# Queries and keys of a mixer take the seven-product form for a third pair of k tiles, with two sets of sums moved earlier

## The chip, the cores and the metric

The kernel runs on one core of one Trainium2 chip, as one launch. The metric is the device time of that launch in microseconds. Each multiplication of the layer is in float32 precision, made on TensorE (PE) out of rounded parts: an operand x is split into a high part (x rounded to fp32r, a cast on ScalarE, ACT) and a low part (x minus the high part, on VectorE, DVE), and a product is summed from three matmuls, high x high, high x low and low x high.

## The reference, cut to what matters

```
x = x + 1/2 * swiglu(rms_norm(x, ffn1_norm), w_gate, w_up, w_down)       # first FFN
h = rms_norm(x, mix_norm);  proj = h @ w_in                              # 256 x 2048 times 2048 x 4112
u, q, k, v, g, a_lr = split(proj, IN_SPLITS)                             # 1024 | 512 | 512 | 1024 | 1024 | 16
x = x + concat(pool(u), gla(q, k, v, g, a_lr)) @ w_out
x = x + cross_attention(rms_norm(x), rms_norm(mem))
x = x + 1/2 * swiglu(rms_norm(x, ffn2_norm), ...);  out = rms_norm(x, final_norm)
```

256 tokens, width 2048, FFN width 5632. The change concerns the end of the first FFN and the 1024 columns q | k of `proj`.

## The kernel before

**Units.** A weight matrix is read in units of 1 MB: 256 rows of k (two "k tiles", called a pair; pairs 0 to 7 cover k = 2048) by 1024 columns. `Stream` keeps a list of units and of operations between them. When unit u is emitted, units up to u + 2 have been split into parts (`AHEAD = 2`), and the split of a unit issues the load of the unit three further on (`RAW = 3` buffers of raw weights). `st.op(f, n)` puts f behind the n-th unit that follows. `in_turn` makes each weight-split instruction of an engine queue behind the one before it; `among_weights` puts other work at a place in that same order, and `issue_after` orders a block behind one instruction.

**Plain and seven-product units.** A plain unit (`unit_p`) is 2 k tiles x 2 column halves x 2 token halves x 3 matmuls = 24 matmuls of 128 x 128 by 128 x 512. Its split is one cast on ACT (wh, 2048 wide) and one subtraction on DVE (wl). A seven-product unit (`unit_s`, `split_seven`) treats the pair as a 2 x 2 block matrix and needs 7 block products of 3 matmuls = 21. For it the raw blocks w0..w3 are added up to four sums in the tile T (three DVE operations, line 488), three raw blocks are split into xh and xl (1536 wide), and the four sums into wh (two casts) and wl. The activations need sums of their own for that pair, made once per pair by `Sums.make` (lines 426 to 438 on DVE, then a cast and a subtraction). The banks of PSUM that hold the seven products' own sums are joined by `combine` (lines 583 to 588) behind the last seven-product unit of a block. PSUM has four tiles (`bufs=4`): a block of `block_s` takes two for its whole sums and two for the parts until `combine` has read them.

**Around the change.** The last part of the first FFN's down product ends with six plain units (`block_t`, columns 1024 to 2047). `into_x` puts behind the first unit that follows: `fold(2)` and `fold(3)`, which transpose the new x on PE (line 802), scale it and split it into `xs` (ACT line 248, DVE line 240) and square it (line 811); one unit later `finish_norm` (sums, Rcol, diag), and `spread_norm` (line 233, two spreads) seven units after the block's end. Then the first mixer block multiplies `xs` by the q | k columns in the order `ORDER_IN = (0, 2, 4, 1, 5, 3, 6, 7)` of pairs, with pairs 1 and 3 in the seven-product form. In what follows u0 to u7 are its eight units in the order of execution; before, u3 (pair 1) and u5 (pair 3) are the seven-product ones. Between u6 and u7 runs the low-rank unit (`low_rank`, line 1077, 16 matmuls into a PSUM tile of its own, `split_a` for its weights). The activations' sums for pairs 1 and 3 are made in the last FFN units, those for pair 5 two units behind the q | k block; they lie in free parts of `ys`. The next block (the pool columns) has again pairs 1 and 3 as seven-product units, and the v and gate blocks have 1, 3 and 5. In the scope of the mixer (`s_mix`) T, xh and xl have one buffer each. The instruction order of each engine is fixed when the program is built, from the order of the code, the constraints named above, and a simulated time.

Of the kernel before, what the change touches and what calls it, by code (L numbers as in the profile page):

```python
# [14 lines left out]
P = 128  # L15
# [5 lines left out]
NB = 512  # L21
# [78 lines left out]
def build(ctx, tc, I, out):  # L100
# [11 lines left out]
    def open_scope(name, shared=None):  # L112


        def f():
            scope["shared"] = shared or {}
            scope["stack"] = ExitStack()
            scope["pool"] = scope["stack"].enter_context(
                tc.tile_pool(name=name, bufs=1, reuse_waits="tile")
            )  # L120
        return f

    def shared_tile(tag, n, dt, name, bufs):

        homes = scope["shared"].get(tag)
        if homes:
            homes.append(homes.pop(0))
            tag, size, bufs = homes[-1]
        else:
            size = n  # L130
        return scope["pool"].tile([P, size], dt, tag=tag, name=name, bufs=bufs)[:, :n]
# [125 lines left out]
    def in_turn(engine, f):  # L257

        if engine in latest:
            with tc.issue_after(latest[engine].ins):  # L260
                latest[engine] = f()
        else:
            latest[engine] = f()
# [6 lines left out]
    def among_weights(f):  # L270
# [4 lines left out]
        if scalar is not None:  # L275
            latest["scalar"] = scalar

    def split_weights(hi, lo, src):
        in_turn("scalar", lambda: nc.scalar.copy(hi, src))  # L279
        in_turn("vector", lambda: nc.vector.tensor_tensor(  # L280
            out=lo, in0=src, in1=f32(hi), op=ALU.subtract
        ))
# [16 lines left out]
    def finish_norm(n, spread_too=True):  # L299

        nc.vector.tensor_reduce(out=sums, in_=ss[:, :, :n], axis=AX.X, op=ALU.add)
        done = rsqrt(Rcol, sums, D, 2)
        if spread_too:
            diag["R"] = [diagonal(Rcol[:, t : t + 1]) for t in range(2)]
        return done
# [60 lines left out]
    def block_t(srcs, act, evict, delays=(0, 0), amid=None):  # L366

        n_k = 2 * len(srcs)  # L370
        held = {}

        def unit(gi):
            def fn(wh, wl):
                if gi == 0:
                    held["ps"] = [ptile(uid("pt")) for _ in range(2)]
                wh, wl = (w.rearrange("p (k j n) -> p k j n", j=2, n=NB) for w in (wh, wl))
                quarters = [(j, kk) for j in range(2) for kk in range(2)]
                if amid is not None and gi == 0:
                    quarters.sort(key=lambda q: q[1])  # L380
                for n, (j, kk) in enumerate(quarters):
                    if amid is not None and n == (1 if gi else 3):
                        amid(gi)
                    k = 2 * gi + kk
                    for h in range(2):
                        products(held["ps"][j][:, h, :], act, k, h, wh[:, kk, j], wl[:, kk, j],
                                 k == 0, k == n_k - 1)
            return fn

        for gi, src in enumerate(srcs):  # L390
            st.unit(src, unit(gi))
        for j in range(2):
            st.op(lambda j=j: evict(j, held["ps"][j]), delays[j])
# [6 lines left out]

    def jtile():
        return tmp.tile([P, NB], F32, tag="j", name=uid("j"))

# [64 lines left out]
        f.clump = True  # L470
        return f

    def split_seven(u, raw, shared):

        t = shared_tile("T", 4 * NB, F32, f"T{u}", 1)
        w = raw.rearrange("p (b n) -> p b n", n=NB)
        v = t.rearrange("p (b n) -> p b n", n=NB)
        th, tl = (
            wpool.tile([P, 4 * NB], F32R, tag=n, name=f"{n}{u}", bufs=st.AHEAD + 1)
            for n in ("wh", "wl")  # L480
        )
        rh, rl = (shared_tile(n, 3 * NB, F32R, f"{n}{u}", 2) for n in ("xh", "xl"))
        for o, a, b in (
            (v[:, 0:2], w[:, 1:3], w[:, 0:1].to_broadcast([P, 2, NB])),
            (v[:, 2], v[:, 0], w[:, 2]),
            (v[:, 3], v[:, 2], w[:, 3]),
        ):
            in_turn("vector", lambda: nc.vector.tensor_tensor(out=o, in0=a, in1=b, op=ALU.add))  # L488
        split_weights(rh, rl, raw[:, NB:])
        for c in (slice(0, 2 * NB), slice(2 * NB, 4 * NB)):  # L490
            in_turn("scalar", lambda: nc.scalar.copy(th[:, c], t[:, c]))  # L491
        low_parts(tl, t, th, shared)
        return [[x.rearrange("p (b n) -> p b n", n=NB) for x in (th, tl, rh, rl)]], None
# [271 lines left out]
    def residual(scale, b, last=1):  # L765

        def evict(j, ps):
            x = x_cols((2 * b + j) * NB, NB)
            nc.vector.scalar_tensor_tensor(
                out=x, in0=ps, scalar=scale, in1=x, op0=ALU.mult, op1=ALU.add  # L770
            )
            if j == last:
                store_x(b)
        return evict
# [57 lines left out]
    END = IntoX((0,), None, None, None)  # L832

    def into_x(w, act, scale, gain=None, k0=0, nk=KT, spread_too=True, src=None, way=OUTPUT,
               spread_at=3, behind=None):

        for b in range(2):
            st.op(lambda b=b: fetch_x(b, src), 2)
            cols = wwide(w, b * 2 * NB, k0, nk)
            if way.sevens[b]:  # L840
                block_s(cols, act, way.sums, way.orders[b], residual(scale, b, 0),
                        early_parts(scale, b), way.sevens[b], behind=None if b else behind)
            else:
                block_t(cols, act, residual(scale, b))
            if gain is not None:
                for j in range(2):
                    st.op(lambda c=2 * b + j: fold(c, gain), way.folds[2 * b + j])
        if gain is not None:
            st.op(lambda: finish_norm(4, spread_too), way.folds[3] + 1)
            if spread_too:  # L850
                st.op(spread_norm, spread_at)

# [99 lines left out]
    def down_first(wd, k0, nk, last, way):  # L952
        way.make_sums()
        if last:
            for g, after in zip(qk_sums.pairs[:2], (9, 11)):
                st.op(lambda g=g: among_weights(lambda: qk_sums.make(g)), after)
        into_x(wd, ys, 0.5, G_MIX if last else None, k0, nk, src=None if k0 else I["x"][0],
               way=way, spread_at=7)

    ffn(I["ffn1_w_gate"][0], I["ffn1_w_up"][0], I["ffn1_w_down"][0], down_first,  # L960
        amid_first)
    st.op(close_scope, 1)
    MIX_HOMES = {"T": [("T", D, 1)], "xh": [("xh", 3 * NB, 1)], "xl": [("xl", 3 * NB, 1)]}
    st.op(open_scope("s_mix", MIX_HOMES), 1)


    w_in = I["w_in"][0]
# [303 lines left out]
    def low_rank():  # L1271
        st.unit(load_a, a_unit, split_a)
        st.op(ev_a)

    block_s(wwide(w_in, 2 * NB), xs, qk_sums, ORDER_IN, ev_qk, home=wide_home, amid={6: low_rank},
            sevens=(1, 3))
    st.op(lambda: turn_qk(1), 1)
    st.op(lambda: turn_qk(0), 2)
    st.op(lambda: among_weights(lambda: qk_sums.make(5)), 2)
    st.op(decay, 2)  # L1280
    def head(h):
        attend(h)
# [6 lines left out]
    def queries_of(*hs):  # L1289
        for h in hs:  # L1290
            st.op(lambda h=h: behind_weights(lambda: queries(h)))

    block_s(wwide(w_in, 0), xs, qk_sums, ORDER_IN, ev_pool, home=wide_home,
            behind={0: (0, decay_logits)}, sevens=(1, 3),
            amid={4: lambda: queries_of(0, 1), 6: lambda: scores_of(0, 1)})
    for f, h, after in (
# [2 lines left out]
        (head, 0, 9), (head, 1, 9), (head, 2, 10), (head, 3, 10), (lambda _: head_norms(), None, 15),  # L1299
    ):  # L1300
        st.op(lambda f=f, h=h: f(h), after)
    def raw_parts_in(high, low):
        of = {n: [(n, 3 * NB, 1), home, (n, 3 * NB, 1)] for n, home in (("xh", high), ("xl", low))}
        return lambda: scope["shared"].update(of)

    st.op(raw_parts_in(("v", 4 * NB, 1), ("m4", 8 * S, 1)))
    block_s(wwide(w_in, 4 * NB), xs, qk_sums, ORDER_IN, ev_v, home=v_home)
    st.op(raw_parts_in(("v", 4 * NB, 1), ("kq", 4 * LINES, 1)))
# [382 lines left out]
    st.op(close_scope)  # L1691


    raws = {}

    def load(u):
        raws[u] = wpool.tile([P, 4 * NB], F32, tag="raw", name=f"raw{u}", bufs=st.RAW)
        st.units[u][0](raws[u])

    def split_unit(u, own, shared):  # L1700
        raw = raws.pop(u)
        if own is split_seven:
            return split_seven(u, raw, shared)
        parts = [
            wpool.tile([P, 4 * NB], F32R, tag=t, name=f"{t}{u}", bufs=st.AHEAD + 1)
            for t in (("wh",) if own else ("wh", "wl"))
        ]
        if own:
            own(parts[0], raw)
            return parts, None  # L1710
        hi, lo = parts
        step = {0: NB, 1: 2 * NB, 2: 2 * NB}.get(u, 4 * NB)
        for c in range(0, 4 * NB, step):
            part = slice(c, c + step)
            if u == 0 and c in (step, 2 * step):
                latest["scalar"] = rows["parts", 0, c // step - 1][0]
            if step < 4 * NB:
                split_weights(hi[:, part], lo[:, part], raw[:, part])
            else:
                in_turn("scalar", lambda: nc.scalar.copy(hi, raw))  # L1720
                low_parts(lo, raw, hi, shared)
        return (hi, lo), None
# [39 lines left out]
```

## Time and profile before

| | |
|---|---|
| time, median of 3 runs | 2072.26 us (2072.12 to 2073.15) |
| the profiled execution's own time | 2072.4 us |
| its span, first to last instruction | 2070.6 us |
| granted TensorE clock, mean | 0.999 |
| matmuls | 9464 |
| VectorE busy / ScalarE busy | 1843.2 us / 1173.4 us |

The profile is one execution, taken by the hardware profiler. A line of a timeline begins with the start and the duration in us, then engine, source line, operation, output and inputs by the program's tile names, their size and the count; what stands in brackets is the engine's idle time before it and what ended it. The chain is the work that ended last, followed back from the end; its pieces follow each other without a gap.

### The profile page before, as it was taken

To read this page: it belongs to the slowest core of one execution; us is meant where nothing else is said; L and a number is where in the kernel's file an instruction comes from. 1 tells how busy PE (TensorE), PEld (TensorE's weight loads), DVE (VectorE), ACT (ScalarE), POOL (GpSimd) and SP (SyncE) were. 2 spreads that over 40 slices of the span, in tenths; PEclk is the share of its full clock that TensorE was granted. 3 is DMA by queue.
4 is the path that set the end of the run, shared out by engine and by line. 5 is a ranking of instruction groups with operands and counts; after the bars stand their busy time and mean duration, and the time that the engine had idled before them with its cause. 6 is when DMAs were issued, how large, how long until landed. Compare 5 with 4: busy or idle time off the path is not lost.

```text
span 2070.6 us, 24069 instructions
## 1 busy us (share of the span) xinstructions
PE 2059.8 (99%) x9464; PEld 1714.1 (83%) x9464; DVE 1843.2 (89%) x1720; ACT 1173.4 (57%) x1196; POOL 103.6 (5%) x93
## 2 busy tenths in 40 slices
PE   9999999999999999999999999999999999999998
PEld 7888888888888888888888888888888888888886
DVE  7998899989998779989889877989988999889987
ACT  7654455554554666665755544656554565545554
POOL 0000000000000000000000000000000010000001
PEclk9999999999999999999999999999999999999999
DMA  7666766566666655467655455666577765676664
GB/s 265 205 203 224 243 214 215 184 228 236 226 201 224 228 182 183 164 205 277 228 183 188 160 181 183 203 224 221 171 238 222 236 213 185 224 242 223 209 226 154
DMA packets 123129, 435.92 MB, mean 211 GB/s; under 512 B 9860, under 2 KB 13544, under 8 KB 122632
## 3 DMA queue, kind: packets, MB, share of 16 engines
q1 hardware_dynamic: 122840, 434.12, 62.6%
q8 instruction: 74, 1.21, 0.2%
q14 instruction: 39, 0.32, 0.0%
q10 hardware_dynamic: 176, 0.27, 0.0%
HBM read 417.58 MB, written 16.78 MB: 210 GB/s over the span
## 4 chain that ended last, share of the span: by engine, by line
PE 99%; DVE 0%; DMA 0%; ACT 0%; issue 0%; SPq 0%; POOL 0%; POOLq 0%; DVEq 0%; ACTq 0%
PE pt L362 64%; PE pt L509 30%; PE ph L791 2%; PE pl L1416 1%; PE pv L1453 1%; PE px L802 1%; PE pp L1049 0%; DMA x<-in_x 0%; PE pa L1077 0%; PE tm L1362 0%; PE po L1215 0%; PE px L728 0%; PE pq L1202 0%; PE pe L362 0%; DVE wl L455 0%
## 5 line engine op out<-in xcount | busy, mean ns | idle before, releaser
L362 PE MATMUL pt<-wh,xs 128*128 128x512 f32 x2432 | 780.9, 391 | 0.0
L1720 ACT CAST wh<-raw 128x2048 fp32r<-128x2048 f32 x242 | 461.7, 1912 | 228.4 <-PE pt L362 128.3
L455 DVE TENSOR_TENSOR wl<-raw,wh 128x2048 fp32r<-128x2048 f32 (+1 forms) x242 | 515.7, 2140 | 82.9 <-ACT wh L1720 82.7
L362 PEld LDWEIGHTS pt<-wh,xs 128*128 128x128 f32 x2432 | 455.9, 188 | 94.4 <-issue 0.5
L491 ACT CAST wh<-T 128x1024 fp32r<-128x1024 f32 x264 | 277.0, 1054 | 380.6 <-DVE T L488 359.6
L362 PE MATMUL pt<-wl,xs 128*128 128x512 f32 x1216 | 474.1, 390 | 0.0
L362 PE MATMUL pt<-wh,ys 128*128 128x512 f32 x1452 | 458.0, 389 | 0.0
L362 PEld LDWEIGHTS pt<-wh,ys 128*128 128x128 f32 x1452 | 272.5, 188 | 56.3
L455 DVE TENSOR_TENSOR wl<-T,wh 128x2048 fp32r<-128x2048 f32 (+1 forms) x132 | 296.7, 2247 | 5.6 <-ACT wh L491 5.2
L362 PE MATMUL pt<-wl,ys 128*128 128x512 f32 x726 | 283.0, 390 | 0.0
L362 PEld LDWEIGHTS pt<-wl,xs 128*128 128x128 f32 x1216 | 228.5, 188 | 46.2
L280 DVE TENSOR_TENSOR xl<-raw,xh 128x1536 fp32r<-128x1536 f32 x132 | 231.1, 1751 | 13.9 <-ACT xh L279 13.8
L279 ACT CAST xh<-raw 128x1536 fp32r<-128x1536 f32 x132 | 195.4, 1480 | 60.6 <-PE pt L509 38.6
L488 DVE TENSOR_TENSOR T<-T,raw 128x512 f32<-128x512 f32 x264 | 182.1, 690 | 6.8
L488 DVE TENSOR_TENSOR T<-raw 128x1024 f32<-128x1024 f32 x132 | 160.7, 1217 | 0.6
L362 PEld LDWEIGHTS pt<-wl,ys 128*128 128x128 f32 x726 | 136.3, 188 | 28.0
L509 PE MATMUL pt<-xh,xs 128*128 128x512 f32 x416 | 154.9, 389 | 0.0
L509 PE MATMUL pt<-wh,xs 128*128 128x512 f32 x396 | 153.9, 389 | 0.0
L459 POOL TENSOR_TENSOR wl<-raw,wh 128x768 fp32r<-128x768 f32 x44 | 81.8, 1858 | 1390.9 <-DVE wl L455 1368.1
L509 PE MATMUL pt<-wh,xe 128*128 128x512 f32 x320 | 124.3, 389 | 0.0
L509 PEld LDWEIGHTS pt<-xh,xs 128*128 128x128 f32 x416 | 78.1, 188 | 16.2
L509 PEld LDWEIGHTS pt<-wh,xs 128*128 128x128 f32 x396 | 74.3, 188 | 15.4
(274 smaller groups left out, 2081.7 us busy)
## 6 DMA issues: line engine op xcount, KB each, us to landing
raw<-in_ffn_w_down SPq DMA_DIRECT2D x88, 1024.0 KB, 5.5
raw<-in_ffn_w_up SPq DMA_DIRECT2D x80, 1024.0 KB, 5.1
raw<-in_ffn_w_gate SPq DMA_DIRECT2D x77, 1024.0 KB, 5.1
raw<-in_w_in SPq DMA_DIRECT2D x32, 1024.0 KB, 5.1
raw<-in_xattn_w_kv SPq DMA_DIRECT2D x32, 1024.0 KB, 5.0
raw<-in_w_out SPq DMA_DIRECT2D x16, 1024.0 KB, 6.6
raw<-in_xattn_w_q SPq DMA_DIRECT2D x16, 1024.0 KB, 5.6
raw<-in_xattn_w_o SPq DMA_DIRECT2D x16, 1024.0 KB, 5.6
```

The costliest lines, as they stand in the source:

```text
L279: in_turn("scalar", lambda: nc.scalar.copy(hi, src))
L280: in_turn("vector", lambda: nc.vector.tensor_tensor(out=lo, in0=src, in1=f32(hi), op=ALU.subtract))
L362: latest["product"] = nc.tensor.matmul(ps, a, w, start=first and i == 0, stop=last and i == 2)
L455: in_turn("vector", lambda: nc.vector.tensor_tensor(out=lo[:, :n], in0=src[:, :n], in1=f32(hi[:, :n]), op=ALU.subtract))
L459: rest = nc.gpsimd.tensor_tensor(out=lo[:, n:], in0=src[:, n:], in1=f32(hi[:, n:]), op=ALU.subtract)
L488: in_turn("vector", lambda: nc.vector.tensor_tensor(out=o, in0=a, in1=b, op=ALU.add))
L491: in_turn("scalar", lambda: nc.scalar.copy(th[:, c], t[:, c]))
L509: nc.tensor.matmul(banks[n], x, w, start=n in fresh and j == 0, stop=n in ends and j == 2)
L791: rows["turned"] = nc.tensor.transpose(v[:, i, h * P : (h + 1) * P], g[:, h, i * P : (i + 1) * P], ident)
L802: nc.tensor.transpose(v[:, j, h * P : (h + 1) * P], x[:, h, j * P : (j + 1) * P], ident)
L1416: nc.tensor.matmul(ps[:, t, :M], ys[:, 4 * h + d, a, tok], xa["K", h][:, d, b, :], start=i == 0, stop=i == 11,)
L1720: in_turn("scalar", lambda: nc.scalar.copy(hi, raw))
```

## The change

1. The q | k block has the order (0, 2, 4, 1, 6, 3, 5, 7) and takes pairs 1, 3 and 5 in the seven-product form, so u4 is pair 6 (plain) and u6 is pair 5 (seven products).
2. The activations' sums for pair 5 are made behind u3 of this block, not two units behind its end.
3. `split_seven` is cut in two: `sum_blocks` (the three additions into T) and the rest. For u3 `sum_blocks` is an operation of its own, ahead of `fold(2)`, `fold(3)` and `finish_norm`, in place of behind them; `finish_norm` is ordered behind it. The scope of the mixer is opened one unit sooner for this.
4. In this block the homes of xh and xl go in turns: their own tile for u3, a part of `ys` for u5, their own tile again for u6.

```diff
@@ shared_tile
             homes.append(homes.pop(0))
+            if callable(homes[-1]):
+                return homes[-1]()
             tag, size, bufs = homes[-1]
@@
+    def behind_sums(f):
+        with tc.issue_after(latest["sums"].ins):
+            f()
@@
-    def split_seven(u, raw, shared):
-        t = shared_tile("T", 4 * NB, F32, f"T{u}", 1)
+    def sum_blocks(u):
+        raw = raws[u]
+        t = block_sums[u] = shared_tile("T", 4 * NB, F32, f"T{u}", 1)
...
         for o, a, b in (
             (v[:, 0:2], w[:, 1:3], w[:, 0:1].to_broadcast([P, 2, NB])),
             (v[:, 2], v[:, 0], w[:, 2]),
             (v[:, 3], v[:, 2], w[:, 3]),
         ):
             in_turn("vector", lambda: nc.vector.tensor_tensor(out=o, in0=a, in1=b, op=ALU.add))
+        latest["sums"] = latest["vector"]
+
+    def split_seven(u, raw, shared):
+        if u not in block_sums:
+            sum_blocks(u)
+        t = block_sums.pop(u)
...
@@ into_x(..., sums_of=None), called with sums_of=3 for the last part of the first FFN
+            if b and sums_of:
+                st.op(lambda u=len(st.units) + sums_of: sum_blocks(u), way.folds[2])
             if gain is not None:
                 for j in range(2):
                     st.op(lambda c=2 * b + j: fold(c, gain), way.folds[2 * b + j])
         if gain is not None:
-            st.op(lambda: finish_norm(4, spread_too), way.folds[3] + 1)
+            norm = lambda: finish_norm(4, spread_too)
+            st.op((lambda: behind_sums(norm)) if sums_of else norm, way.folds[3] + 1)
@@
-    st.op(close_scope, 1)
+    st.op(close_scope)
...
-    st.op(open_scope("s_mix", MIX_HOMES), 1)
+    st.op(open_scope("s_mix", MIX_HOMES))
@@
-    block_s(wwide(w_in, 2 * NB), xs, qk_sums, ORDER_IN, ev_qk, home=wide_home, amid={6: low_rank},
-            sevens=(1, 3))
+    def raw_parts_in_ys():
+        return raw_parts_in(*(
+            lambda i=i: ys[:, 3 * i : 3 * i + 3].rearrange("p k a s -> p (k a s)") for i in range(2)
+        ))
+
+    def third_sums():
+        st.op(lambda: among_weights(lambda: qk_sums.make(5)))
+
+    st.op(raw_parts_in_ys())
+    block_s(wwide(w_in, 2 * NB), xs, qk_sums, (0, 2, 4, 1, 6, 3, 5, 7), ev_qk, home=wide_home,
+            amid={3: third_sums, 6: low_rank})
     st.op(lambda: turn_qk(1), 1)
     st.op(lambda: turn_qk(0), 2)
-    st.op(lambda: among_weights(lambda: qk_sums.make(5)), 2)
     st.op(decay, 2)
@@ ahead of the pool block
+    st.op(lambda: scope["shared"].update({n: [(n, 3 * NB, 1)] for n in ("xh", "xl")}))
@@ split_unit (raws now stands further up)
-        raw = raws.pop(u)
+        raw = raws[u]
```

More of the change, by code (lines that the diff above doesn't have):

```diff
@@ L393, in block_t @@
             st.op(lambda j=j: evict(j, held["ps"][j]), delays[j])
+    raws = {}
     def jtile():
@@ L471, in clump @@
         return f
-    def split_seven(u, raw, shared):
-        t = shared_tile("T", 4 * NB, F32, f"T{u}", 1)
+    block_sums = {}
+    def sum_blocks(u):
+        raw = raws[u]
+        t = block_sums[u] = shared_tile("T", 4 * NB, F32, f"T{u}", 1)
         w = raw.rearrange("p (b n) -> p b n", n=NB)
         v = t.rearrange("p (b n) -> p b n", n=NB)
[L478 to L482, printed above, removed]
         for o, a, b in (
@@ L488, in split_seven @@
             in_turn("vector", lambda: nc.vector.tensor_tensor(out=o, in0=a, in1=b, op=ALU.add))
+        latest["sums"] = latest["vector"]
[3 more added lines that the diff above has]
+        t = block_sums.pop(u)
+        th, tl = (
+            wpool.tile([P, 4 * NB], F32R, tag=n, name=f"{n}{u}", bufs=st.AHEAD + 1)
+            for n in ("wh", "wl")
+        )
+        rh, rl = (shared_tile(n, 3 * NB, F32R, f"{n}{u}", 2) for n in ("xh", "xl"))
         split_weights(rh, rl, raw[:, NB:])
@@ L834, in into_x @@
     def into_x(w, act, scale, gain=None, k0=0, nk=KT, spread_too=True, src=None, way=OUTPUT,
-               spread_at=3, behind=None):
+               spread_at=3, behind=None, sums_of=None):
         for b in range(2):
@@ L957, in down_first @@
         into_x(wd, ys, 0.5, G_MIX if last else None, k0, nk, src=None if k0 else I["x"][0],
-               way=way, spread_at=7)
+               way=way, spread_at=7, sums_of=3 if last else None)
     ffn(I["ffn1_w_gate"][0], I["ffn1_w_up"][0], I["ffn1_w_down"][0], down_first,
         amid_first)
-    st.op(close_scope, 1)
+    st.op(close_scope)
     MIX_HOMES = {"T": [("T", D, 1)], "xh": [("xh", 3 * NB, 1)], "xl": [("xl", 3 * NB, 1)]}
-    st.op(open_scope("s_mix", MIX_HOMES), 1)
+    st.op(open_scope("s_mix", MIX_HOMES))
     w_in = I["w_in"][0]
@@ L1273, in low_rank, with raw_parts_in @@
         st.op(ev_a)
-    block_s(wwide(w_in, 2 * NB), xs, qk_sums, ORDER_IN, ev_qk, home=wide_home, amid={6: low_rank},
-            sevens=(1, 3))
+    def raw_parts_in(high, low):
+        of = {n: [(n, 3 * NB, 1), home, (n, 3 * NB, 1)] for n, home in (("xh", high), ("xl", low))}
+        return lambda: scope["shared"].update(of)
+    def raw_parts_in_ys():
[7 more added lines that the diff above has]
+            amid={3: third_sums, 6: low_rank})
     st.op(lambda: turn_qk(1), 1)
     st.op(lambda: turn_qk(0), 2)
-    st.op(lambda: among_weights(lambda: qk_sums.make(5)), 2)
     st.op(decay, 2)
@@ L1301, in build @@
         st.op(lambda f=f, h=h: f(h), after)
-    def raw_parts_in(high, low):
-        of = {n: [(n, 3 * NB, 1), home, (n, 3 * NB, 1)] for n, home in (("xh", high), ("xl", low))}
-        return lambda: scope["shared"].update(of)
     st.op(raw_parts_in(("v", 4 * NB, 1), ("m4", 8 * S, 1)))
@@ L1691, in build @@
     st.op(close_scope)
-    raws = {}
     def load(u):
```

## The prediction

> **What bounds the kernel now.** I read the page first: the busy shares and the chain of work that ended last.
>
> ```profile
> PE 2059.8 (99%) x9464; PEld 1714.1 (83%) x9464; DVE 1843.2 (89%) x1720; ACT 1173.4 (57%) x1196; POOL 103.6 (5%) x93
> PE 99%; DVE 0%; DMA 0%; ACT 0%; issue 0%; SPq 0%; POOL 0%; POOLq 0%; DVEq 0%; ACTq 0%
> ```
>
> The chain is TensorE alone, and a busy TensorE could still hide stretched matmuls; so I read the pieces of the chain around the q | k block next (start, duration, what), to compare each piece with its count.
>
> ```profile
> 714.38 10.93 PE pt L362 x48
> 725.31 2.72 PE pt L509 x12
> ...
> 730.29 5.21 PE pt L362 x23
> 735.51 2.72 PE pt L509 x12
> ...
> 740.49 5.21 PE pt L362 x23
> 745.71 0.45 PE ps L233 x4
> 746.15 0.47 PE pt L362 x2
> 746.62 3.63 PE pa L1077 x16
> 750.25 7.71 PE pt L362 x34
> ...
> 775.52 4.76 PE pt L509 x21
> 780.28 5.44 PE pt L362 x24
> ```
>
> Every piece is its count times one pitch: 5.44 / 24 = 0.2267 us, 4.76 / 21 = 0.2267, 10.93 / 48 = 0.2277. So u0 to u7 run with no wait at all: u1 and u2 (x48), u3 with seven products, u4 plain, u5 with seven, u6 plain, the spreads, two matmuls of u7, the low-rank unit, the rest of u7. TensorE has nothing to gain from an earlier input; it only gains from fewer matmuls, and loses if an input comes late. Which inputs are near their limit is told by the busy time of the engines by stage (window, length, then PE, PEld, DVE, ACT, POOL, clock, DMA share, GB/s):
>
> ```profile
> 709.00:725.00 16.00, 16.00 (x80) 13.45 (x80) 13.62 (x24) 12.73 (x23) 0.00 (x0) 1.00 0.55 189
> 725.00:735.00 10.00, 10.00 (x46) 8.29 (x45) 9.93 (x7) 5.19 (x4) 0.00 (x0) 1.00 0.60 173
> 735.00:745.00 10.00, 10.00 (x46) 8.29 (x45) 6.55 (x7) 2.82 (x3) 0.00 (x0) 1.00 0.65 235
> ```
>
> VectorE is full from 725 to 735 us and idle for 2.4 and 3.4 us in the windows around it. The change adds VectorE work just here, so its queue is the one to follow:
>
> ```profile
> 709.21 2.29 DVE L455 TENSOR_TENSOR wl<-raw,wh 128x2048 fp32r<-128x2048 f32 x1 [0.28 <-ACT wh L1720]
> 712.10 0.16 DVE L301 TENSOR_REDUCE sums<-ss 128x2 f32<-128x8 f32 x1 [0.59 <-ACT j L811]
> ...
> 713.61 0.17 DVE L216 RECIPROCAL Rcol<-chain 128x2 f32<-128x2 f32 x1 [1.15 <-ACT chain L215]
> ...
> 715.15 3.22 DVE L240 SCALAR_TENSOR_TENSOR xs<-px,gains,xs 128x256 fp32r<-128x256 f32 x8 [0.18 <-ACT xs L248]
> 718.29 1.21 DVE L488 TENSOR_TENSOR T<-raw 128x1024 f32<-128x1024 f32 x1
> ...
> 720.87 1.75 DVE L280 TENSOR_TENSOR xl<-raw,xh 128x1536 fp32r<-128x1536 f32 x1
> 722.54 2.28 DVE L455 TENSOR_TENSOR wl<-T,wh 128x2048 fp32r<-128x2048 f32 x1
> 724.74 2.29 DVE L455 TENSOR_TENSOR wl<-raw,wh 128x2048 fp32r<-128x2048 f32 x1
> ...
> 735.67 1.22 DVE L1070 TENSOR_SCALAR wh<-ident 128x2048 fp32r<-128x2048 f32 x1
> 737.40 0.43 DVE L286 TENSOR_TENSOR wh<-raw,wh 128x256 fp32r<-128x256 f32 x1 [0.52 <-ACT wh L285]
> 740.70 0.69 DVE L584 TENSOR_TENSOR rows<-pt,rows 128x512 f32<-128x512 f32 x1 [2.87 <-ACT rows L583]
> 741.42 1.23 DVE L585 TENSOR_TENSOR rows<-pt,rows 128x1024 f32<-128x1024 f32 x1
> 742.68 0.69 DVE L588 TENSOR_TENSOR rows<-pt,rows 128x512 f32<-128x512 f32 x1
> 743.29 2.28 DVE L455 TENSOR_TENSOR wl<-raw,wh 128x2048 fp32r<-128x2048 f32 x1
> ```
>
> ```profile
> 740.57 1.92 ACT L1720 CAST wh<-raw 128x2048 fp32r<-128x2048 f32 x1
> ```
>
> The reader is to see how close u3 is: its xl begins at 720.87, its wl ends at 722.54 + 2.28 = 724.82, and TensorE starts u3 at about 725.1. The last VectorE row is the wl of u7; ScalarE's cast for it, the last row, ended at 742.5.
>
> **The change part by part.** *The matmuls.* u6 becomes a seven-product unit: 24 - 21 = 3 matmuls and their weight loads go. By the two pieces above, 5.44 - 4.76 = 0.68 us, on the path that sets the end. Nothing else on TensorE is added. The Trainium skill (TensorE: Matmul & The Clock Gate, "Wait — 56ns, not 53.3ns?") gives a start-to-start time of N ÷ 2.4 GHz plus about 2.5 ns, 215.7 ns at N = 512, an estimate of 0.65 us for three; the rows' 226.7 ns is the longer and decides.
>
> *VectorE, added and moved.* From start to start the steps cost: additions into T 720.87 - 718.29 = 2.58, xl 722.54 - 720.87 = 1.67, a wl 724.74 - 722.54 = 2.20. A seven-product unit is therefore 6.45, a plain one 2.20: u6 costs 4.25 more. The pair's activation sums are read where they stand now:
>
> ```profile
> 767.15 0.68 DVE L426 TENSOR_TENSOR j<-xs 128x512 f32<-128x512 f32 x1
> ...
> 768.52 0.29 DVE L435 SCALAR_TENSOR_TENSOR j<-j 128x128 f32<-128x128 f32 x1
> ...
> 779.85 0.68 DVE L286 TENSOR_TENSOR ys<-j,ys 128x512 fp32r<-128x512 f32 x1
> ```
>
> One operation, four small ones (the first and the third of them begin 768.52 - 767.15 = 1.37 into it with 0.33 between them) and the subtraction: 0.68 + 4 x 0.33 + 0.68, about 2.7 us, that leave the pool block and come ahead of u6's split. So 4.25 + 2.7 = 6.95 us are added between 709 and 745 us. The windows have 2.4 + 0.1 + 3.4 = 5.9 us of idle there: on average it does not fit. But the idle time is not a bound on its own, since what counts is when each product is due; the queue worked out in order, from 709.21: wl of u2 to 711.41; the moved additions of u3 to 713.99; `finish_norm` (712.10 to 715.15 less its waits of 1.15 and 0.18, so 1.7) and the eight low parts of the folds (718.29 - 715.15 = 3.14) to 718.8; xl of u3 to 720.5, its wl to 722.7 (before 724.8, so the moved additions buy 2.1 us); wl of u4 724.9; u5's three steps 731.4; the sums of pair 5 734.1; u6's additions 736.6, xl 738.3, wl 740.5; the low-rank weights (1.22 + 0.43) 742.2 (and 744.4 if the next wl followed at once); wl of u7, whose cast can come no later than before, since u5 frees its buffer at the same time, from 742.5 to 744.7.
>
> Against this stand the due times, which TensorE sets: u6 starts at about 740.3 (740.49 less one pitch). Its products P1, P2 and P3 read xl from the second matmul, 740.5, and P7 reads wl from the eleventh, 742.6. u7 follows at 740.3 + 4.76 = 745.0 and reads its wl at 745.3. The margins are 2.2, 2.1 and 0.6 us. So the 6.95 us lie beside TensorE's work; what hides them is that units are split two ahead, and if the margin of 0.6 is gone the cost is what the queue is late beyond it.
>
> *The other queues.* ScalarE gains an xh cast of 1.5 us for u6 (the row below; the two halves of its wh cast are together as wide as the plain one) in a stretch where it is busy 2.82 of 10 us: beside. The wait that the xh cast of u5 has now,
>
> ```profile
> 727.84 1.49 ACT L279 CAST xh<-raw 128x1536 fp32r<-128x1536 f32 x1 [3.98 <-PE pt L509]
> ```
>
> goes, because u5's parts have a home in `ys`; nothing on TensorE waited for it. SyncE's loads follow the splits:
>
> ```profile
> 700.61 5.85 SPq L638 DMA_DIRECT2D raw<-in_w_in  x2
> ```
>
> ```profile
> raw<-in_w_in SPq DMA_DIRECT2D x32, 1024.0 KB, 5.1
> ```
>
> The first of these two is u3's load (by the page's median of 5.1 us to landing it is there at 705.7), well ahead of the additions at 711.4. The load behind u6's split moves from about 735.7 to 738.3; it lands at 743.4, and the split that reads it is not due before u6 ends at 745.0. No DMA is added.
>
> *What the added waits hold up.* The additions now stand in VectorE's queue ahead of the folds' low parts: these begin at 714.0 to 715.7 in place of 715.15, and u2 (pair 4, the first reader of fold 2) starts on TensorE at 714.38 + 10.93 / 2 = 719.8: 2 us or more to spare. `combine` now follows u6, with spreads and low-rank unit right behind; see the first rival.
>
> **Sum.** The profiled execution: 2072.4 - 0.68 = 2071.7, its span 2070.6 - 0.7 = 2069.9, with 1.8 us outside the span as before. It lies 0.1 above the median of the runs; against that median, 2072.26 - 0.68 = **2071.6 us**.
>
> **The rivals.** *1. PSUM, slower than before.* All four PSUM tiles are held until `combine` reads the parts. Before, that happened under the plain u6; now the spreads and the low-rank unit, which need a tile each, come right behind the last seven-product unit. The rows that time it, beside the VectorE rows above:
>
> ```profile
> 740.08 0.59 ACT L583 COPY rows<-pt 128x512 f32<-128x512 f32 x1 [2.71 <-PE pt L509]
> ```
>
> u5 ends at about 740.26; the first parts tile is free at 740.70 + 0.69 = 741.4, 1.1 us later, the second at 742.68 + 0.69 = 743.4, 3.1 us later. If the built order puts spreads and low-rank unit straight behind u6, TensorE stands for 1.1 us, and again for 3.1 - 1.1 - 0.45 = 1.55 us: 2.65 in all, net +1.97, so 2074.2 us. It decides if u7's matmuls aren't placed in that gap. Against it: the chain shows two matmuls of u7 between the spreads and the low-rank unit, so the order is made by what is ready, and u7's own weights are ready at 744.7. The Trainium skill (TensorE: Matmul & The Clock Gate, "The mechanism" in Part 3) has matmuls in strict program order, by which a spread at the head would hold all of u7 back; the trace shows no such wait.
>
> *2. VectorE late.* The idle waits of the quoted rows in this stretch (0.28 + 0.59 + 1.15 + 0.18 + 0.52 = 2.7 us) come back in full, since the order is fixed beforehand and `finish_norm` still waits for ScalarE's square root. Then the queue reaches the end of u7's wl at 744.4 + 2.7 = 747.1, 1.8 us after 745.3; net +1.1, so 2073.4. A second way to the same end: with the scope opened sooner, T (the scope's first tile) may lie where the FFN still holds rows of x, whose last stores are these (issue, then the landing of the two):
>
> ```profile
> 708.96 0.81 SPq L763 DMA_DIRECT2D X<-x  x2
> DMA to landing us min/median/max: 3.8/4.2/4.7
> ```
>
> The additions would then wait until 709.8 + 4.7 = 714.5, 3.1 us later, and u7's wl would end 2.2 us late: net +1.5, so 2073.8. For this rival: VectorE at 9.93 of 10 us already. Against it: in the code T is the first tile of its scope as the x rows of the columns 0 to 1023 were of theirs, and those were stored a block earlier; and between 715.15 and 735.67 the quoted rows show no idle time, so waits are rare while VectorE has a backlog.
>
> *3. It doesn't do what it says.* The three matmuls go, but as much is given back in switches between transposes, spreads and fp32r matmuls (the x48 piece is 10.93 - 48 x 0.2267 = 0.05 long): 2072.3. And of the part that moves the additions: TensorE shows no wait at u3 now, so by itself it brings nothing.
>
> **How the numbers follow.** Forecast 0.76, rival 1 0.10, rival 2 0.08, rival 3 0.03, and 0.03 for more than one stall together or something unseen. The range goes from 2070.7 (the forecast less the 0.9 us by which the highest run before lies above the median) to 2073.8, which takes in both forms of rival 2 and rival 3 and leaves rival 1's full price out. A difference under 0.2%, 4.1 us, is about what a measurement of this kernel can't tell from no change. Forecast and all three rivals lie inside it; only several stalls together reach beyond: faster 0.02, within 0.94, slower 0.04.
>
> **What would show it.** In the changed profile: 9461 matmuls; u6 as a piece of 21 at 4.76 us and no piece longer than its count; the three additions of u3 ahead of the folds' low parts; the wl of u7 ending by 745.3 and matmuls of u7 ahead of the low-rank unit's. Wrong would be a TensorE gap behind u6 named after lines 584 to 588 (rival 1) or 455 (rival 2), or a time outside 2070.7 to 2073.8.

## The result and the profile after

| | before | after |
|---|---|---|
| median of the runs | 2072.36 us (2071.85 to 2073.44, 22 runs) | 2076.18 us (2074.65 to 2077.46, 22 runs) |
| profiled execution, and its span | 2072.4 us, 2070.6 us | 2077.33 us, 2075.6 us |
| granted clock, mean | 0.999 | 0.998 |

The ratio is 1.0018, 95% interval 1.0012 to 1.0023: 3.8 us slower, where 0.7 us less was forecast, and above the top of the range (2073.8). The page of the changed kernel has the same balance of engines, and one share that was 0 in the chain before:

```profile
PE 2061.2 (99%) x9461; PEld 1714.9 (83%) x9461; DVE 1846.5 (89%) x1724; ACT 1175.3 (57%) x1198; POOL 103.6 (5%) x93
PE 98%; DVE 1%; ACT 0%; DMA 0%; issue 0%; SPq 0%; POOL 0%; POOLq 0%; DVEq 0%; ACTq 0%
```

The three matmuls are gone (9461). DVE's 1% of the chain is new, so the chain's pieces come next (start, duration, what), from the folds' transposes on. Line numbers have moved: plain units' matmuls are L369 (before 362), seven-product ones L527 (509), wl L464 (455), the low-rank unit L1098 (1077), the logits of the decay, which read its result aT, L1114 (1093).

```profile
713.56 1.75 PE px L820 x16
...
736.65 7.25 PE pt L527 x32
743.91 0.23 PE pt L369
744.13 2.04 PE pt L527 x9
746.17 5.21 PE pt L369 x23
...
751.83 3.64 PE pa L1098 x16
755.48 8.16 PE pt L369 x36
763.63 0.23 PE pt L527
763.86 1.92 PE pz L1114 x8
765.78 2.98 PE pt L369 x12
...
781.41 2.30 DVE wl L464
783.75 6.89 PE pt L369 x22
```

Three things are to be seen. The q | k block has no gap: around u6 (pieces x32, x1 and x9) every piece is its count times 0.227 us. The spreads now run behind 23 matmuls of u7, where they stood ahead of u7, and the low-rank unit right behind the spreads, where it had two matmuls of u7 ahead of it; the logits stand 36 + 1 matmuls behind the low-rank unit, before 34. And 12 matmuls behind the logits, at 768.76, the chain leaves TensorE: it goes through ScalarE and VectorE to a wl that TensorE waits for at 783.75, in the **pool** block, 38 us behind u6. TensorE's timeline has the gap, and in brackets what ended it:

```profile
780.58 0.39 PE L527 MATMUL pt<-wh,ys 128*128 128x512 f32 x1
783.75 0.50 PE L369 MATMUL pt<-wl,xs 128*128 128x512 f32 x1 [2.78 <-DVE wl L464]
```

From start to start it is 783.75 - 780.58 = 3.17 us in place of 0.23, so 2.94 us are lost. What ScalarE and VectorE did before it, from their timelines:

```profile
765.82 1.57 ACT L1121 ACTIVATE m<-pz,gains 128x256 f32<-128x256 f32 x4 [4.29 <-PE pz L1114]
768.78 2.00 ACT L509 CAST wh<-T 128x1024 fp32r<-128x1024 f32 x2 [0.30 <-PE pt L369]
```

```profile
757.04 0.40 DVE L1108 TENSOR_TENSOR aT<-pa,c 32x256 f32<-32x256 f32 x1
757.72 2.29 DVE L464 TENSOR_TENSOR wl<-raw,wh 128x2048 fp32r<-128x2048 f32 x1 [0.28 <-ACT wh L1748]
759.93 0.40 DVE L1109 TENSOR_TENSOR aT<-aT,R 32x256 f32<-32x256 f32 x1
...
776.46 1.23 DVE L1130 SCALAR_TENSOR_TENSOR m<-m 128x1024 f32<-128x1024 f32 x1 [3.35 <-ACT m L1129]
777.79 2.44 DVE L1134 TENSOR_TENSOR_SCAN m<-keep,m 128x256 f32<-128x256 f32 x4
...
781.41 2.29 DVE L464 TENSOR_TENSOR wl<-raw,wh 128x2048 fp32r<-128x2048 f32 x1
```

ScalarE stands idle 4.29 us until the logits come (line 1121 reads them), and then 0.30 us more for TensorE before a cast of weights that is ahead of the decay's logarithm (line 1129) in its order; this second wait is why the chain leaves TensorE 12 matmuls behind the logits. The wl itself is not late for lack of data: it stands in the fixed order behind the decay's steps on VectorE (m, lines 1130 to 1141), and VectorE waits 3.35 us idle for that logarithm. The rows of before to compare, of TensorE's chain, VectorE's timeline and TensorE's timeline:

```profile
712.63 1.75 PE px L802 x16
...
757.95 1.92 PE pz L1093 x8
```

```profile
751.12 0.41 DVE L1088 TENSOR_TENSOR aT<-aT,R 32x256 f32<-32x256 f32 x1
771.56 1.23 DVE L1109 SCALAR_TENSOR_TENSOR m<-m 128x1024 f32<-128x1024 f32 x1 [2.74 <-ACT m L1108]
776.51 2.28 DVE L455 TENSOR_TENSOR wl<-raw,wh 128x2048 fp32r<-128x2048 f32 x1
```

```profile
780.34 0.39 PE L362 MATMUL pt<-wl,xs 128*128 128x512 f32 x1
```

Two profiles start up differently, so I count from the px piece on. The low-rank unit starts 38.3 us behind it, before 746.62 - 712.63 = 34.0; aT is complete at 46.8, before 38.9; the logits start at 763.86 - 713.56 = 50.3, before 45.3; the decay's work on VectorE at 62.9, before 58.9; the wl at 67.85, before 63.88. So the wl is 3.97 us late. Before, it ended at 778.79 and was first read by the second matmul of its unit, at 780.34 (the last row), so it had 1.55 us to spare. In the changed kernel three matmuls fewer come ahead of that reader and one more of its own unit does, so it is due 2 x 0.227 = 0.45 us sooner. 3.97 - 1.55 + 0.45 = 2.87 us of gap, beside 2.94 measured.

The gap has a sequel, in a window of what follows (window, length, then PE, PEld, DVE, ACT, POOL, clock, DMA share, GB/s):

```profile
785.00:788.40 3.40, 3.40 (x9) 2.64 (x8) 3.40 (x5) 1.84 (x2) 0.00 (x0) 0.50 0.81 298
```

For 3.4 us the granted clock is 0.50: eight matmuls there start 0.427 us apart in place of 0.227, which is 8 x 0.2 = 1.6 us. So: -0.68 + 2.94 + 1.6 = +3.9 us. From the first px matmul to the end of the span the trace has 1362.16 us, before 1358.14: **+4.02**, beside +3.8 in the medians. Whether the clock falls in each of the 22 runs is not shown, since one execution is profiled, the third longest of them; the five shortest, 2074.65 to 2075.13 us, lie near 2072.36 - 0.68 + 2.94 = 2074.6, the sum without the low clock.

### The profile page after: what moved, and what is told of

The parts are those of the page before. It is cut to its first block, busy times and chain, and to the rows that moved or that the text cites. A ratio compares the mean times of both kernels' runs of the same rounds, so it can differ in the third digit from the quotient of the medians.

```text
span 2075.6 us, 24067 instructions
## 1 busy us (share of the span) xinstructions
PE 2061.2 (99%) x9461; PEld 1714.9 (83%) x9461; DVE 1846.5 (89%) x1724; ACT 1175.3 (57%) x1198; POOL 103.6 (5%) x93
## 4 chain that ended last, share of the span: by engine, by line
PE 98%; DVE 1%; ACT 0%; DMA 0%; issue 0%; SPq 0%; POOL 0%; POOLq 0%; DVEq 0%; ACTq 0%
PE pt L369 63%; PE pt L527 30%; PE ph L809 1%; PE pl L1446 1%; PE pv L1483 1%; PE px L820 1%; DMA x<-in_x 0%; PE pp L1070 0%; DVE wl L464 0%; ACT wh L509 0%; PE pa L1098 0%; PE tm L1392 0%; PE po L1236 0%; PE px L746 0%; PE pq L1223 0%
## 5 line engine op out<-in xcount | busy, mean ns | idle before, releaser
L369 PE MATMUL pt<-wh,xs 128*128 128x512 f32 x2416 | 776.5, 391 | 0.0
L464 DVE TENSOR_TENSOR wl<-raw,wh 128x2048 fp32r<-128x2048 f32 (+1 forms) x241 | 513.5, 2139 | 81.5 <-ACT wh L1748 81.3
L369 PEld LDWEIGHTS pt<-wh,xs 128*128 128x128 f32 x2416 | 453.7, 188 | 93.7 <-issue 0.5
L369 PE MATMUL pt<-wl,xs 128*128 128x512 f32 x1208 | 472.0, 391 | 2.8 <-DVE wl L464 2.8
L369 PE MATMUL pt<-wh,ys 128*128 128x512 f32 x1452 | 458.0, 389 | 0.0
L369 PEld LDWEIGHTS pt<-wh,ys 128*128 128x128 f32 x1452 | 272.5, 188 | 56.1
L464 DVE TENSOR_TENSOR wl<-T,wh 128x2048 fp32r<-128x2048 f32 (+1 forms) x133 | 299.0, 2248 | 10.6 <-ACT wh L509 10.2
L369 PE MATMUL pt<-wl,ys 128*128 128x512 f32 x726 | 283.0, 390 | 0.0
L369 PEld LDWEIGHTS pt<-wl,xs 128*128 128x128 f32 x1208 | 227.5, 188 | 49.6 <-DVE wl L464 3.2
L369 PEld LDWEIGHTS pt<-wl,ys 128*128 128x128 f32 x726 | 136.3, 188 | 28.1
L527 PE MATMUL pt<-xh,xs 128*128 128x512 f32 x416 | 154.9, 389 | 0.0
L527 PE MATMUL pt<-wh,xs 128*128 128x512 f32 x398 | 154.7, 389 | 0.0
L527 PE MATMUL pt<-wh,xe 128*128 128x512 f32 x320 | 124.3, 389 | 0.0
L527 PEld LDWEIGHTS pt<-xh,xs 128*128 128x128 f32 x416 | 78.1, 188 | 16.2
L527 PEld LDWEIGHTS pt<-wh,xs 128*128 128x128 f32 x398 | 74.7, 188 | 15.5
```

The source lines that it names most:

```text
L369: latest["product"] = nc.tensor.matmul(ps, a, w, start=first and i == 0, stop=last and i == 2)
L464: in_turn("vector", lambda: nc.vector.tensor_tensor(out=lo[:, :n], in0=src[:, :n], in1=f32(hi[:, :n]), op=ALU.subtract))
L527: nc.tensor.matmul(banks[n], x, w, start=n in fresh and j == 0, stop=n in ends and j == 2)
```

## The experiments

The theory after this reading, **A**: what is late is the low-rank unit (it needs PSUM tiles that `combine` frees, now behind u6), then aT, the logits and the decay's chain on VectorE, and the wl queued behind it. The rival, **B**: VectorE has 4.25 + 2.7 us more to do for the third pair and is behind until the pool block. A third reading is that moving pair 5's sums out of the pool block, or the homes in `ys`, did it. That PSUM holds the low-rank unit back is inferred from the code and from times: the built order has filled the place with u7's matmuls, so the trace names no wait there. The last steps on VectorE for the unit's weights and for `combine` in the changed kernel are:

```profile
740.10 0.42 DVE L293 TENSOR_TENSOR wh<-raw,wh 128x256 fp32r<-128x256 f32 x1
748.36 0.69 DVE L606 TENSOR_TENSOR rows<-pt,rows 128x512 f32<-128x512 f32 x1
```

The weights were ready at 740.52, 11 us before the unit started, so they did not hold it back; `combine` had read the parts at 749.05, 2.8 us before. Intervals are 95%. "px to end" is the trace from the first px matmul to the end of the span (before 1358.14, after 1362.16), which leaves out the start of the kernel, whose length differs between runs.

### Before, with the low-rank unit late

```diff
-    block_s(..., ORDER_IN, ev_qk, home=wide_home, amid={6: low_rank},
+    block_s(..., ORDER_IN, ev_qk, home=wide_home, amid={7: low_rank},
             sevens=(1, 3))
```

> The kernel before, with one edit: the low-rank unit runs behind u7 in place of behind u6. Pairs 1 and 3 alone have seven products, nothing else is moved. Theory A (what costs time in the changed kernel is that the low-rank unit comes some 5 us later, and with it the gate's logits, the ScalarE and VectorE work on them, and the wl of the pool block's fifth unit, which stands behind that work in VectorE's queue): a TensorE gap of about 3 us ahead of a plain unit at about 780 us, the granted clock at 0.5 for about 3.4 us behind it in some runs as in the changed kernel (984.97 - 980 there: 784.97 to 788.38), 2072.4 + 2.9 = 2075.3 without and about 2077.0 with the low clock. Theory B (the VectorE work that was added for the third pair, 7 us, runs late into the pool block): no gap, 2072.4, since none of that work is added here.

Measured: 2077.81 us (7 runs), 1.0026 of before (1.0015 to 1.0036). The chain of its profile:

```profile
753.05 3.63 PE pa L1077 x16
756.67 8.33 PE pt L362 x36
765.23 1.92 PE pz L1093 x8
...
783.13 2.21 DVE wl L455
785.39 5.28 PE pt L362 x22
```

The same chain and the same wait, 3.21 us at the same unit, with no third seven-product unit and no VectorE work added. B is not needed for the gap. The low-rank unit is 753.05 - 714.08 = 39.0 us behind px, and px to end is 1362.12 us: +3.98, the gap and about 0.7 us of short waits behind it. A's sums of 2075.3 and 2077.0 were too low; the start of this execution was 1.4 us longer too. A surprise on the side: in this profile the clock did not fall behind the gap.

```profile
787.00:792.00 5.00, 5.00 (x23) 3.85 (x22) 5.00 (x7) 3.21 (x4) 0.00 (x0) 1.00 0.51 195
```

This run's mean clock is listed as 0.999, that of the other six as 0.997 or 0.998, so it may have fallen in those.

### After, with aT's two steps at a place in the order of the weight splits

```diff
-        nc.vector.tensor_tensor(out=t, in0=t, in1=rows["R"][:32, :], op=ALU.mult)
+        return None, nc.vector.tensor_tensor(out=t, in0=t, in1=rows["R"][:32, :], op=ALU.mult)
...
-        st.op(ev_a)
+        st.op(lambda: among_weights(ev_a))
```

> The changed kernel, with one edit: the two additions that turn the low-rank unit's product into aT take their place among VectorE's weight splits, so no wl comes between them (in the changed kernel they start at 757.04 and 759.93) and the logits' matmuls can stand 24 matmuls sooner in TensorE's order. Theory A: the logits come about 5 us sooner, the gap at 780 us goes, the clock stays at 1.0; what is left is the three matmuls saved, 2072.4 - 0.7 = 2071.7. Theory B: the VectorE work is the same, so the gap stays and the time is 2075 to 2077.

Measured: 2071.90 us (11 runs), 0.9996 of before (0.9987 to 1.0005). Its chain:

```profile
711.78 1.75 PE px L820 x16
...
744.40 5.21 PE pt L369 x23
...
750.05 3.64 PE pa L1098 x16
753.70 2.94 PE pt L369 x13
756.64 1.92 PE pz L1114 x8
...
778.74 5.44 PE pt L369 x24
```

The low-rank unit is as late as in the changed kernel (750.05 - 711.78 = 38.3 us behind px) and still behind 23 matmuls of u7, but the two steps that make aT (an addition and, second, a multiplication by the row factor R) now follow each other:

```profile
754.13 0.41 DVE L1108 TENSOR_TENSOR aT<-pa,c 32x256 f32<-32x256 f32 x1 [3.61 <-ACT c L1107]
754.58 0.41 DVE L1109 TENSOR_TENSOR aT<-aT,R 32x256 f32<-32x256 f32 x1
```

The logits come 13 matmuls behind the unit (44.9 us behind px, before 45.3), the piece of the gap is whole again (x24, 5.44), the clock stays at 1.00. B falls: all the VectorE work of the third pair is in this kernel. And theory A has to be narrowed: the unit's own lateness of 4.3 us is affordable, because before there were 757.95 - 751.53 = 6.4 us between aT and the logits. In the changed kernel the logits stood 37 matmuls behind the unit, so its 4.3 us and three matmuls more, 5.0 us in all, came through to them, although aT had been complete for 763.86 - 760.33 = 3.5 us. What costs is the place that the built order gave the logits. That it gave them this place because of the wl between aT's two steps is likely, since with this edit both are gone, but it is not shown by itself. In the first experiment, too, a wl stood between the two steps (at 759.55 and 763.22) and the logits 37 matmuls behind the unit, so that run does not part the unit's lateness from the order.

The same kernel again, beside the later runs:

> The kernel of e2 once more, for its size: three matmuls of 0.227 us less than before and no gap, so 0.7 us (0.03%) under the runs of before beside it. Rival: no difference from before.

Measured: 2071.99 us (11 runs), 0.9998 of before (0.9989 to 1.0007). The lead over before isn't resolved by the times; the traces have it. Px to end is 1357.48 and 1357.47 us in the two profiles, 0.66 and 0.67 less than before: three matmuls, and nothing else.

### After, with the decay one unit later

```diff
-    st.op(decay, 2)
+    st.op(decay, 3)
```

> The changed kernel, with one edit: the decay (logarithm, scan and difference of the gate) is put one unit later, so that the wl of the pool block's fifth unit stands ahead of it in VectorE's queue. The logits stay as late as in the changed kernel. Theory A: the plain fifth unit no longer waits; the next unit, with seven products, now has its additions behind the decay and may be up to 1 us late: 2071.7 to 2072.7. Theory B: the work on VectorE is the same and only in another order, so the gap moves to the next unit: 2074 to 2077.

Measured: 2074.59 us (10 runs), 1.001 of before (1.0001 to 1.0019). The gap goes from its old place and comes back at the next unit, a seven-product one, where xl now stands behind the decay:

```profile
787.91 1.68 DVE xl L287
789.64 3.17 PE pt L527 x8
```

It is 2.13 us long, and the clock is at 0.50 behind it in the profiled execution, as the window there shows:

```profile
790.40:793.80 3.40, 3.40 (x9) 2.68 (x9) 3.40 (x2) 3.08 (x8) 0.00 (x0) 0.50 0.88 292
```

That execution took 2077.36 us, the longest of the ten; the median has +1.85 over before, and -0.68 + 2.13 = +1.45 without the low clock, so the median run need not have had it. The result is what B had forecast here, and A's figure was missed: A put the wait at the next unit at up to 1 us, and it was 2.13. Taken alone this run would speak for B, and the first two experiments decide against it. What it does show is that the chain's place in VectorE's order sets which unit waits.

### After, with pair 5 plain in this block

```diff
-            amid={3: third_sums, 6: low_rank})
+            amid={3: third_sums, 6: low_rank}, sevens=(1, 3))
```

> The changed kernel with u6 (pair 5) plain; order of pairs, early activation sums of pair 5, moved additions and the homes in ys stay. The sums of the seven-product parts are then joined under u6 again and the low-rank unit has its PSUM tile on time. Theory A: no gap, TensorE's work as before the change, 2072.4. Theory B: 4.25 of the 6.95 us of VectorE work are gone but the 2.7 us of activation sums are still there; no gap or a small one, 2072.4 to 2073.4.

Measured: 2072.39 us (10 runs), 0.9999 of before (0.999 to 1.0008). `combine` is behind u5 again, and with it the low-rank unit is behind two matmuls of u7 as before:

```profile
747.20 0.47 PE pt L369 x2
747.67 3.63 PE pa L1098 x16
```

Px to end is 1358.14, as before to the last digit. In this trace the sooner sums, the sooner scope and the pool block without pair 5's sums cost nothing and bring nothing without a third seven-product unit, so the third reading falls. B's forecast took this time in too, so the run does not part A from B.

### After, with the seven-product units one place sooner

```diff
-    block_s(..., (0, 2, 4, 1, 6, 3, 5, 7), ev_qk, ...)
+    block_s(..., (0, 2, 4, 1, 3, 5, 6, 7), ev_qk, ...)
```

> The changed kernel with one edit: the order of pairs (0, 2, 4, 1, 3, 5, 6, 7), so the three seven-product units are u3, u4, u5 and the plain u6 stands between the last of them and the low-rank unit. All the added VectorE work is there, and a little closer together. Theory A (the parts' PSUM tiles, which are read out behind the last seven-product unit, hold the low-rank unit back): the low-rank unit runs under u7's first matmuls as before the change, no gap at 780 us; VectorE reaches the wl of u5 at about 738.3 where it is due at 737.2, so a gap of 0 to 2 us at u4 or u5: 2071.7 to 2073.7. Theory B (the third seven-product unit's VectorE work): the gap at 780 us stays, 2075 to 2077.

Measured: 2078.26 us (7 runs), 1.0028 of before (1.0017 to 1.0038). Both forecasts were missed. Here the third seven-product unit is u5, and what the PSUM reading says of the order holds: the chain has again two matmuls between spreads and low-rank unit, and no wait in the pool block. But now VectorE really is late:

```profile
737.36 2.28 DVE wl L464
741.79 0.63 ACT ys L292
```

```profile
742.20:745.60 3.40, 3.13 (x7) 2.48 (x8) 2.37 (x2) 0.21 (x1) 0.00 (x0) 0.50 0.91 311
```

Two gaps, 2.09 us at 737.4 and 1.97 us at 740.3, then the clock at 0.50 again. The first is for u5's wl, the second for pair 5's sums. I had put the queue about 1 us late and had not seen that the low-rank weights come ahead of that wl in VectorE's order and wait 1.18 us for TensorE, nor that pair 5's sums come behind it. With the order of the forecast TensorE has no wait in the block; one place sooner and it has.

### After with aT's steps in place, less one part of the change

Two more take the better kernel (the second experiment) and undo one part. First, u3's block sums back behind the folds:

```diff
-               way=way, spread_at=7, sums_of=3 if last else None)
+               way=way, spread_at=7)
...
-    st.op(close_scope)
+    st.op(close_scope, 1)
...
-    st.op(open_scope("s_mix", MIX_HOMES))
+    st.op(open_scope("s_mix", MIX_HOMES), 1)
...
-    st.op(raw_parts_in_ys())
+    st.op(raw_parts_in_ys(), 1)
```

> The kernel of e2 with u3's additions back behind the folds and finish_norm, and the mixer's scope opened where it was before. Theory: the moved additions buy VectorE 2.1 us, and u7's wl ended 745.5 in the changed kernel with u7 starting at 746.0, so without them it comes about 1.4 us late: 2071.9 + 1.4 = 2073.3, with the gap ahead of u7. Rival: the queue has slack that the sum didn't see, or the built order puts other work there; no gap, 2071.9.

Measured: 2072.40 us (10 runs), 1.0000 of before (0.9991 to 1.0009), beside 2071.99 with the sums moved. Px to end is 1358.25, 0.77 more than with them. TensorE waits 0.19 and 0.33 us at u6, not at u7 as expected. The first is for its xl, the second for its wl, which ends at 743.43.

Then, one home for xh and xl:

```diff
-    st.op(raw_parts_in_ys())
     block_s(...)
```

> The kernel of e2 with xh and xl in their one tile each for u3, u5 and u6, none in ys. Theory: the cast of u6's xh waits until u5's last matmul has read the tile, then 1.5 us of cast and 1.7 us of subtraction stand ahead of u6: a gap of about 3 us there, 2071.9 + 3 = 2074.9, and up to 1.7 us more in runs whose clock falls to 0.5 behind the gap: 2076.6. Rival: other units' matmuls fill the gap, 2071.9 to 2073.

Measured: 2073.06 us (10 runs), 0.9999 of before (0.999 to 1.0009), so not told apart from it; the median is 1.07 us above the kernel with two homes, measured beside it, and px to end is 1358.71, 1.2 us more than there. The waits at u6 are 0.62 and 0.35 us, a third of what was expected. ScalarE's timeline has why:

```profile
737.94 1.49 ACT L286 CAST xh<-raw 128x1536 fp32r<-128x1536 f32 x1 [1.14 <-PE pt L527]
```

u6's cast waits for readers of u5's xh on TensorE, but starts well ahead of u5's end: only products P1 to P3 read xh and xl, the first nine matmuls of the unit, so the tile is free some 2.7 us before the unit is done.

## Why the prediction was wrong

**Right: the three matmuls.** 0.68 us forecast; with the new wait taken out, the two traces of the second experiment are 0.66 and 0.67 us shorter than before.

**Right: VectorE's margins in the block, the term that looked most dangerous.** In the changed kernel's timeline:

```profile
738.44 1.75 DVE L287 TENSOR_TENSOR xl<-raw,xh 128x1536 fp32r<-128x1536 f32 x1
740.44 2.29 DVE L464 TENSOR_TENSOR wl<-T,wh 128x2048 fp32r<-128x2048 f32 x1
743.22 2.29 DVE L464 TENSOR_TENSOR wl<-raw,wh 128x2048 fp32r<-128x2048 f32 x1 [0.49 <-ACT wh L1748]
```

They end at 740.19, 742.73 and 745.51. In TensorE's timeline u6 starts at 741.03, and their first readers at 741.93, 743.97 and 746.24: margins of 1.7, 1.2 and 0.7 us, forecast 2.2, 2.1 and 0.6. The prediction had xl read by u6's second matmul and wl by its eleventh; they are read by its fifth and thirteenth. Rival 2 did not come about. The moved sums and the second home earn their place with 0.8 and 1.2 us from px to end, mostly waits at u6 (0.19 + 0.33 and 0.62 + 0.35 us).

**Right in its mechanism: rival 1's escape.** The four PSUM tiles were held until `combine` behind u6, and u7's matmuls were placed in the gap: 23 of them, and no wait behind u6.

**Wrong: "it decides if u7's matmuls aren't placed in that gap".** This is the step that failed. I priced the later release of PSUM only as a stall of TensorE at that spot, and took it for nothing once the spot is filled. But work that is put in front puts back what stood there. The low-rank unit was 4.3 us later, aT 7.9, the logits 5.0, the decay's scans 4.0, and behind these in VectorE's fixed order stood a wl with 1.55 us to spare. The prediction even named matmuls of u7 ahead of the low-rank unit's as a sign of being right; they came, and they are the start of the loss. The part on what the added waits hold up named the two blocks behind `combine` and stopped there; who waits for aT was not asked. The profile of before had the two slacks for that question: 6.4 us between aT and the logits, and 1.55 us at the pool block's fifth unit. What it could not have told is that the built order would part aT's two steps and leave the logits 37 matmuls behind the unit; the second experiment shows that with another order the unit's lateness costs nothing. Why the order, which is made from a simulated time, came out so was not tried.

**Missing: the clock.** The forecast's costs were lengths of gaps. Behind this gap the clock was at 0.50 for 3.4 us in the profiled execution, 1.6 us more, so even with the gap seen the sum would have been -0.68 + 2.94 = +2.3 of the +3.9. The Trainium skill (TensorE: Matmul & The Clock Gate, "HAM oscillation — how this bites in real kernels") asks for no idle gaps over about 3.4 us. The trace disagrees: 2.94 us, and 2.13 in the third experiment, were enough, while 3.21 us in the first showed no drop.

**The range** went to 2073.8 because it was built from two rivals that both end inside the q | k block. The signs named as wrong looked at the same place; of them only the time outside the range came true. What happened falls under the 0.03 left for something unseen. The 4.1 us given there as about what can't be told from no change was too much: the 3.8 us came with an interval of 2.5 to 4.8 us.

## What to carry to other kernels

If an edit makes a tile's last reader later, list what waits for that tile and follow it, in the order of each engine, to the next piece of work with a deadline; a gap that other work fills has only been handed on. A short chain that many things depend on (here two steps of 0.4 us) deserves an explicit place in a built order: here a 2.3 us operation stood between its halves, and an explicit place took the gap away. Where TensorE sets the end, price a gap of 2 to 3 us without and with the clock's reaction (1.6 us here).

The changed kernel with aT's two steps placed among the weight splits has the lowest medians seen, 2071.90 and 2071.99 us: it beats the changed kernel clearly, and the kernel before by three matmuls in the trace, though not beyond the uncertainty of the times.

## What the runs showed of the hardware

The granted clock fell to 0.50 for one stretch of 3.4 us behind idle gaps of 2.94 us (after), 2.13 us (decay later) and 2.09 + 1.97 us (sevens sooner); behind one of 3.21 us (low-rank late) it did not in the profiled run. It begins 1.3 us after work resumes (after), 0.8 us (decay later), and as the second gap ends (sevens sooner). The stretch agrees in length with the window of about 3.4 us in the Trainium skill (TensorE: Matmul & The Clock Gate, Part 1); what in a gap decides whether it comes isn't settled by these runs. In it the matmuls' pitch rises from 0.227 to 0.427 us, a little less than double.
